# A decayed running sum over a matrix product: five of eight column slots solved pairwise with help from ScalarE and GpSimd

## The chip, the cores and the metric

The kernel runs on one core of one Trainium2 chip. The metric is device time of one execution in microseconds (us); lower is better. Engines in the profile's names: PE is TensorE (PEld its weight loads), DVE is VectorE, ACT is ScalarE, POOL is GpSimd, SP is SyncE, which only issues transfers here.

## The reference

x has 16 sequences of 2048 rows of 1024 numbers, w is 1024 x 1024, decay has one factor per column, all in fp32.

```python
def reference(x, w, decay):
    B, S, D = x.shape                 # 16, 2048, 1024
    xw = x @ w
    out = np.zeros_like(xw)
    out[:, 0, :] = xw[:, 0, :].copy()
    for t in range(1, S):
        out[:, t, :] = decay[None, :] * out[:, t - 1, :] + xw[:, t, :]
    return out.astype(np.float32)
```

Each output column is a recurrence over the 2048 rows of a sequence: the new value is the decay times the last one plus an element of the matrix product.

## The kernel before

A *chunk* is 512 rows of one sequence (64 chunks in all). The columns are handled with a row index t along the free dimension and columns along the 128 partitions, four blocks of 32 columns (one of each quarter of the 1024, index q) making up a *slot* n; there are 8 slots (K = 8), and also 8 blocks of the contraction, index k.

- `load` (L103) brings a chunk of x from memory on GpSimd's queue, cast to bf16 on the way, in four pieces of 256 KB, one per quarter q, into one of four xb buffers.
- `turn` (L112) transposes the chunk on VectorE in 32 x 32 blocks, as fp32 words that hold two bf16, into xt (four buffers), so that the contraction lies on the partitions.
- `load_w` (L77 to L90) loads w in fp32 on SP's and ScalarE's queues, and the decay behind it on the same two queues (L82); VectorE casts the even k into wsb, ScalarE the odd ones.
- `matmul` (L129): for each slot and chunk, 8 matmuls of 128 x 128 weights by 512 columns accumulate into a PSUM tile ps. PSUM has four tiles of 1024 fp32 per partition.
- `scan` (L141): VectorE runs the recurrence over the whole tile with one scan instruction, from PSUM into so. Its initial value is the last element of the tile before, which ScalarE copies to `keep` (L151).
- `back` (L156): VectorE transposes so in 32 x 32 blocks into the output tile ot (two buffers), so that rows lie on the partitions again. The back of a slot is put off until after the next slot's scan (`pending`, `flush`).
- `store` (L166): when all 8 slots of a group are in ot, SP issues four transfers, one per quarter, of 1024 KB each.

The work is done in *groups*: two groups of a single chunk, 30 groups of two chunks, two groups of a single chunk. In a two-chunk group a tile is 1024 rows long, and each slot has 16 matmuls. The next group's two chunks are turned after the scans of slots 1 and 5, and behind each turn one more chunk is loaded. In group 0 the loop over k is outside of the one over slots, so that matmuls can start when the first block of w is there. The order on each engine is the program's, except where the language's scheduler moves an instruction; nothing is pinned.

Of the kernel before, what the change touches and what calls it, by code (L numbers as in the profile page):

```python
# [9 lines left out]
FP32 = mybir.dt.float32  # L10
BF16 = mybir.dt.bfloat16
ALU = mybir.AluOpType


def _ap(ap_obj: bass.AP, new_ap, extra_offset=0):
    return dataclasses.replace(
        ap_obj,
        ap=[list(p) for p in new_ap],
        offset=ap_obj.offset + extra_offset,
    )  # L20
# [4 lines left out]
@with_exitstack  # L25
def kernel(
    ctx: ExitStack,
    tc: tile.TileContext,
    x: bass.AP,
    w: bass.AP,  # L30
    decay: bass.AP,
    out: bass.AP,
):

    nc = tc.nc
    B, S, D = x.shape
    assert w.shape == (D, D)

    NQ = 4
    P = 32
    CQ = D // NQ  # L50
    K = CQ // P
    M = K // 2
    TL = 512
    NJ = TL // P
    NC = S // TL

    const = ctx.enter_context(tc.tile_pool(name="const", bufs=1))
    xbp = ctx.enter_context(tc.tile_pool(name="xbp", bufs=4))
    xtp = ctx.enter_context(tc.tile_pool(name="xtp", bufs=4))
    sop = ctx.enter_context(tc.tile_pool(name="sop", bufs=3))  # L60
    otp = ctx.enter_context(tc.tile_pool(name="otp", bufs=2))
    psp = ctx.enter_context(tc.tile_pool(name="psp", bufs=4, space=bass.MemoryType.PSUM))

    def quad(q):
        return slice(q * P, (q + 1) * P)

    def queue(q):
        return nc.sync if q < 2 else nc.scalar

    dec = const.tile([128, K], FP32, name="dec")  # L70
    wsb = const.tile([128, K, K, NQ, P], BF16, name="wsb")

    def load_w():
        wf = otp.tile([128, M, 2 * D], FP32, name="ot")
        for m in range(M):
            for q in (0, 2, 1, 3):
                queue(q).dma_start(  # L77
                    out=wf[quad(q), m],
                    in_=_ap(w, [[2 * D, P], [1, 2 * D]], (q * CQ + m * 2 * P) * D))
        with nc.allow_non_contiguous_dma(reason="a vector of 1024"):  # L80
            for q in range(NQ):
                queue(q).dma_start(  # L82
                    out=dec[quad(q), :], in_=_ap(decay, [[1, P], [P, K]], q * CQ))
        for k in range(K):
            dst = wsb[:, k].rearrange("p n q i -> p q n i")
            src = wf.rearrange("p m (e q n i) -> p (m e) q n i", e=2, q=NQ, n=K)[:, k]
            if k % 2:
                nc.scalar.copy(out=dst, in_=src)  # L88
            else:
                nc.vector.tensor_copy(out=dst, in_=src)  # L90

    chunks = [(b, c * TL) for b in range(B) for c in range(NC)]
    nch = len(chunks)
    xt_of = {}
    xb_of = {}

    def load(c):
        if c >= nch:
            return
        b, t0 = chunks[c]  # L100
        xb = xbp.tile([128, NJ, CQ], BF16, name="xb")
        for q in range(NQ):
            nc.gpsimd.dma_start(  # L103
                out=xb[quad(q)],
                in_=_ap(x, [[D, P], [P * D, NJ], [1, CQ]], (b * S + t0) * D + q * CQ))
        xb_of[c] = xb

    def turn(c):
        xt = xtp.tile([128, M, TL, 2], BF16, name="xt")
        src = xb_of.pop(c).rearrange("p j c -> p (j c)").bitcast(FP32)  # L110
        dst = xt.rearrange("p m t e -> p (m t e)").bitcast(FP32)
        nc.vector.transpose(  # L112
            out=dst.rearrange("p (m j i) -> p j m i", m=M, i=P),
            in_=src.rearrange("p (j m c) -> p j m c", m=M, c=P))
        xt_of[c] = xt

    groups = [[0], [1]] + [[c, c + 1] for c in range(2, nch - 2, 2)] + [[nch - 2], [nch - 1]]
    for g in groups:
        assert chunks[g[0]][0] == chunks[g[-1]][0]

    last = {}
    pending = []

    def flush():
        while pending:
            pending.pop(0)()

    def matmul(ps, n, k, xt):
        nc.tensor.matmul(  # L129
            out=ps,  # L130
            lhsT=wsb[:, k, n].rearrange("p q i -> p (q i)"),
            rhs=xt[:, k // 2, :, k % 2],
            start=(k == 0),
            stop=(k == K - 1),
        )

    def scan(g, n, ps, ot):
        b, t0 = chunks[g[0]]
        T = TL * len(g)
        so = sop.tile([128, T], FP32, name="so")  # L140
        nc.vector.tensor_tensor_scan(  # L141
            out=so,
            data0=dec[:, n:n + 1].to_broadcast([128, T]),
            data1=ps,
            initial=0.0 if t0 == 0 else last[n],
            op0=ALU.mult,
            op1=ALU.add,
        )
        if t0 + T < S:
            keep = const.tile([128, 1], FP32, name=f"keep{n}", bufs=2)  # L150
            nc.scalar.copy(out=keep, in_=so[:, T - 1:T])  # L151
            last[n] = keep
        flush()

        def back():
            nc.vector.transpose(  # L156
                out=ot[:, :, n * P:(n + 1) * P],
                in_=so.rearrange("p (i t) -> p i t", t=P))

        pending.append(back)  # L160

    def store(g, ot, n0, n1, queues):
        b, t0 = chunks[g[0]]
        T = TL * len(g)
        for q in (0, 2, 1, 3):
            queues(q).dma_start(  # L166
                out=_ap(out, [[D, P], [P * D, T // P], [1, (n1 - n0) * P]],
                        (b * S + t0) * D + q * CQ + n0 * P),
                in_=ot[quad(q), :, n0 * P:n1 * P])

    load(0)
    load_w()
    load(1)
    load(2)
    load(3)
    turn(0)
    next_load = 4
    for gi, g in enumerate(groups):
        T = TL * len(g)
        ot = otp.tile([128, T // P, CQ], FP32, name="ot")  # L180
        xts = [xt_of.pop(c) for c in g]
        after = groups[gi + 1] if gi + 1 < len(groups) else []
        at = {1: after[:1], 5: after[1:]}
        final = gi + 1 == len(groups)
        if len(g) == 1:
            pss = [psp.tile([128, 2, TL], FP32, name="ps") for _ in range(K // 2)]
            if gi == 0:
                order = [(n, k) for k in range(K) for n in range(K)]
            else:
                order = [(n, k) for n in range(K) for k in range(K)]  # L190
            for n, k in order:
                matmul(pss[n // 2][:, n % 2], n, k, xts[0])
        for n in range(K):
            if len(g) == 1:
                ps = pss[n // 2][:, n % 2]
            else:
                ps = psp.tile([128, T], FP32, name="ps")
                for k in range(K):
                    for l in range(2):
                        matmul(ps[:, l * TL:(l + 1) * TL], n, k, xts[l])  # L200
            scan(g, n, ps, ot)
            for c in at.get(n, []):
                turn(c)
                load(next_load)
                next_load += 1
            if final and n == K // 2:
                pending.append(lambda: store(g, ot, 0, K // 2, queue))
        if final:
            flush()
            store(g, ot, K // 2, K, queue)  # L210
        else:
            pending.append(lambda g=g, ot=ot: store(g, ot, 0, K, lambda q: nc.sync))


# [28 lines left out]
```

## Time and profile before

| | us |
|---|---|
| time, median of 3 runs (lowest to highest) | 1050.16 (1049.74 to 1050.61) |
| the profiled execution | 1049.7 |
| its span, first to last instruction | 1047.9 |
| busy: PE, DVE | 934.0, 1000.2 |
| busy: ACT, POOL | 32.7, 163.4 |
| mean granted TensorE clock (share of full) | 0.987 |
| bytes moved by DMA, mean rate | 206.19 MB, 197 GB/s |

Busy time is the time in which an engine executed something; matmuls overlap one another, so a busy PE is not a PE at its peak, and the distance between the starts of two neighbours says more than the duration of one. Lines of the profile name the source line, the engine, the operation and the tiles (output <- inputs), and for a group of instructions the count, the busy time, the mean duration, and the idle time in front of them with what ended it.

### The profile page before, as it was taken

Reading aid. Unit: us, or ns where it says so; the run is one execution under the profiler, and the core shown is the slowest. Engines: PE = TensorE matmul, PEld = TensorE weight load, DVE = VectorE, ACT = ScalarE, POOL = GpSimd, SP = SyncE. Lnnn points to the kernel's source line nnn. Section 1 sums busy time; section 2 is a strip of 40 time slices with the busy share of each in tenths; the row PEclk is TensorE's granted clock in tenths of the full one; section 3 lists DMA queues with packets and bytes.
Section 4 is the critical chain, followed back from the end, with each engine's and each line's share of the span. In section 5 each row is a group of like instructions: output and inputs, shape, how many; then the busy total and the mean of one; then the engine's idle time right before and its main releaser. Section 6 shows DMA issues by size and latency. Waiting matters only on the chain.

```text
span 1047.9 us, 9953 instructions
## 1 busy us (share of the span) xinstructions
PE 934.0 (89%) x4015; PEld 391.9 (37%) x4096; DVE 1000.2 (95%) x612; ACT 32.7 (3%) x149; POOL 163.4 (16%) x260
## 2 busy tenths in 40 slices
PE   0869999999999999999999999999999999999990
PEld 0324444433333443333443333344333344333340
DVE  0699999999999999999999999999999999999995
ACT  1000000000000000000000000000000000000000
POOL 2401111101111100111101111110111110010000
PEclk9989999999999999999999999999999999999996
DMA  9998997999999999999999999999999999998558
GB/s 212 185 167 158 186 223 159 207 204 222 207 190 196 200 204 211 215 201 190 197 203 207 223 199 195 190 206 204 220 210 192 195 198 204 206 220 182 132 128 221
DMA packets 272430, 206.19 MB, mean 197 GB/s; under 512 B 7680, under 2 KB 271872, under 8 KB 271872
## 3 DMA queue, kind: packets, MB, share of 16 engines
q1 hardware_dynamic: 134176, 135.28, 54.9%
q0 software_dynamic: 135168, 67.13, 48.4%
q10 hardware_dynamic: 3040, 3.15, 1.3%
q8 instruction: 32, 0.52, 0.2%
q14 instruction: 14, 0.11, 0.0%
HBM read 138.42 MB, written 134.22 MB: 260 GB/s over the span
## 4 chain that ended last, share of the span: by engine, by line
DMA 51%; DVE 22%; issue 17%; POOL 6%; PE 3%; DVEq 0%; SPq 0%; POOLq 0%
DMA xb<-in_x_dram 50%; DVE ot L156 9%; DVE xt L112 7%; POOL xb L103 6%; DVE so L141 5%; PE ps L129 3%; DMA out_dram<-ot 2%; SPq L166 0%; DVEq L156 0%; DVEq L112 0%; POOLq L238 0%; DVEq L238 0%; DVEq L141 0%; POOLq L227 0%
## 5 line engine op out<-in xcount | busy, mean ns | idle before, releaser
L129 PE MATMUL ps<-xt,wsb 128*128 128x512 bf16 x4015 | 934.0, 388 | 90.2 <-DVE so L141 54.2
L129 PEld LDWEIGHTS <-wsb 128*128 128x128 bf16 x4096 | 391.9, 96 | 631.8 <-issue 100.9
L156 DVE STREAM_TRANSPOSE ot<-so 128x1024 f32<-128x1024 f32 (+1 forms) x272 | 316.0, 1175 | 6.0 <-DMA out_dram<-ot 5.9
L141 DVE TENSOR_TENSOR_SCAN so<-dec,keep,ps 128x1024 f32<-128x1024 f32 (+1 forms) x144 | 309.9, 2155 | 1.1 <-PE ps L129 1.1
L141 DVE TENSOR_TENSOR_SCAN so<-dec,ps 128x1024 f32<-128x1024 f32 (+1 forms) x128 | 282.5, 2209 | 3.5 <-PE ps L129 3.5
L103 POOL DMA_DIRECT2D xb<-in_x_dram x256 | 163.2, 645 | 762.3 <-DVE xt L112 731.9
L112 DVE STREAM_TRANSPOSE xt<-xb 128x2048 f32<-128x2048 f32 x64 | 145.8, 2301 | 18.5 <-DMA xb<-in_x_dram 18.5
L151 ACT COPY keep<-so 128x1 f32<-128x1 f32 x144 | 27.6, 191 | 969.8 <-DVE so L141 969.8
L90 DVE CAST wsb<-ot 128x1024 bf16<-128x1024 f32 x4 | 2.6, 680 | 12.0 <-DMA ot<-in_w_dram 12.0
L88 ACT CAST wsb<-ot 128x1024 bf16<-128x1024 f32 x4 | 3.9, 1041 | 0.0
L88 ACT ACT_TABLE_LOAD x1 | 1.3, 1283 | 17.5 <-DMA ot<-in_w_dram 17.5
L227 POOL MEMSET const-float32-0.0<- 128x1 f32 x1 | 0.1, 98 | 0.2 <-issue 0.2
L227 POOL MEMSET const-bfloat16-1.0<- 128x1 bf16 x1 | 0.1, 101 | 0.0
L227 POOL MEMSET const-float32-1.0<- 128x1 f32 x1 | 0.1, 98 | 0.0
L227 POOL MEMSET const-uint8-127<- 128x1 uint8 x1 | 0.1, 98 | 0.0
## 6 DMA issues: line engine op xcount, KB each, us to landing
out_dram<-ot SPq DMA_DIRECT2D x120, 1024.0 KB, 15.2
xb<-in_x_dram POOLq DMA_DIRECT2D x256, 256.0 KB, 18.8
out_dram<-ot SPq DMA_DIRECT2D x12, 512.0 KB, 8.1
ot<-in_w_dram ACTq DMA_DIRECT2D x8, 256.0 KB, 8.9
ot<-in_w_dram SPq DMA_DIRECT2D x8, 256.0 KB, 8.7
out_dram<-ot SPq DMA_DIRECT2D x4, 256.0 KB, 3.3
out_dram<-ot ACTq DMA_DIRECT2D x4, 256.0 KB, 4.0
dec<-in_decay_dram SPq DMA_DIRECT2D x2, 1.0 KB, 7.6
```

Source lines behind the costliest of these rows:

```text
L88: nc.scalar.copy(out=dst, in_=src)
L90: nc.vector.tensor_copy(out=dst, in_=src)
L103: nc.gpsimd.dma_start(out=xb[quad(q)], in_=_ap(x, [[D, P], [P * D, NJ], [1, CQ]], (b * S + t0) * D + q * CQ))
L112: nc.vector.transpose(out=dst.rearrange("p (m j i) -> p j m i", m=M, i=P), in_=src.rearrange("p (j m c) -> p j m c", m=M, c=P))
L129: nc.tensor.matmul(out=ps, lhsT=wsb[:, k, n].rearrange("p q i -> p (q i)"), rhs=xt[:, k // 2, :, k % 2], start=(k == 0), stop=(k == K - 1),)
L141: nc.vector.tensor_tensor_scan(out=so, data0=dec[:, n:n + 1].to_broadcast([128, T]), data1=ps, initial=0.0 if t0 == 0 else last[n], op0=AL ...
L151: nc.scalar.copy(out=keep, in_=so[:, T - 1:T])
L156: nc.vector.transpose(out=ot[:, :, n * P:(n + 1) * P], in_=so.rearrange("p (i t) -> p i t", t=P))
L227: nc = _bacc.Bacc("TRN2", target_bir_lowering=False, num_devices=1)
```

## The change

The recurrence is y[t] = d y[t-1] + v[t]. For five of the eight slots (n = 0, 1, 3, 4, 6; not in the last group) it is solved in pairs: with z = d v[even] + v[odd], the odd elements follow y[odd] = d^2 y[odd before] + z, a scan of half the length, and the even ones follow from them, y[even] = d y[odd before] + v[even].

- ScalarE copies the PSUM tile to xs in SBUF and writes its even elements times d to h; GpSimd adds h to the odd elements of xs; VectorE scans these 512 with d^2, which lies in PSUM (`dec2`), into every second element of so.
- Then ScalarE multiplies the scanned elements by d, and GpSimd adds the even elements of xs into the gaps of so.
- The paired slot's scan is issued one slot later, its back two slots later. The other three slots scan from PSUM as before.
- so has four buffers instead of three and two elements more in front; PSUM has three tiles of 1024 instead of four, and one tile for d^2. In group 0 only the slots 0 to 5 run with k outside; 6 and 7 follow.
- w is loaded on GpSimd's queue, behind chunk 0, and cast to bf16 by the transfer; the casts on VectorE and ScalarE become bf16 copies that reorder it. decay is loaded on ScalarE's queue, in the program behind its casts; its square is computed on VectorE in front of turn(0).
- Pieces of x are issued one or, while more than four wait, two per slot, from a list (`loads`); the turns come after slots 1 and 4.
- Every instruction but the stores' transfers is pinned: each engine's order is that of the program.

```diff
+    pin = tc.keep_in_program_order
+    PAIRED = (0, 1, 3, 4, 6)
+    TURNS = (1, 4)
-    psp = ctx.enter_context(tc.tile_pool(name="psp", bufs=4, space=bass.MemoryType.PSUM))
+    psp = ctx.enter_context(tc.tile_pool(name="psp", bufs=3, space=bass.MemoryType.PSUM))
+    pdp = ctx.enter_context(tc.tile_pool(name="pdp", bufs=1, space=bass.MemoryType.PSUM))
...
+    dec2 = pdp.tile([128, 512], FP32, name="dec2")
...
+    def load_dec():
...
+            for q in range(NQ):
+                pin(nc.scalar.dma_start(
+                    out=dec[quad(q), :], in_=_ap(decay, [[1, P], [P, K]], q * CQ)))
+        pin(nc.vector.tensor_tensor(out=dec2[:, 0:K], in0=dec, in1=dec, op=ALU.mult))
...
     def load_w():
-        wf = otp.tile([128, M, 2 * D], FP32, name="ot")
+        wb = otp.tile([128, M, 2 * D], BF16, name="ot")
         for m in range(M):
-            for q in (0, 2, 1, 3):
-                queue(q).dma_start(
-                    out=wf[quad(q), m],
+            for q in range(NQ):
+                pin(nc.gpsimd.dma_start(
+                    out=wb[quad(q), m],
...
+        def decayed(self, src):
+            h = tmp.tile([128, self.T // 2], FP32, name="h", bufs=4)
+            pin(nc.scalar.activation(
+                out=h, in_=src, func=mybir.ActivationFunctionType.Copy,
+                scale=dec[:, self.n:self.n + 1]))
+            return h
+
+        def pair(self):
+            if not self.paired:
+                return
+            T = self.T
+            self.xs = tmp.tile([128, T], FP32, name="xs", bufs=3)
+            pin(nc.scalar.copy(out=self.xs, in_=self.ps))
+            g = self.decayed(self.ps[:, 0:T:2])
+            if self.prev is None:
+                pin(nc.gpsimd.memset(self.so[:, 1:2], 0.0))
+            else:
+                pin(nc.scalar.copy(out=self.so[:, 1:2], in_=self.prev))
+            pin(nc.gpsimd.tensor_tensor(
+                out=self.xs[:, 1:T:2], in0=g, in1=self.xs[:, 1:T:2], op=ALU.add))
+
+        def scan(self):
+            T, n, so = self.T, self.n, self.so
+            if self.paired:
+                pin(nc.vector.tensor_tensor_scan(
+                    out=so[:, 3:T + 2:2],
+                    data0=dec2[:, n:n + 1].to_broadcast([128, T // 2]),
+                    data1=self.xs[:, 1:T:2],
+                    initial=0.0 if self.prev is None else self.prev,
...
+            else:
+                pin(nc.vector.tensor_tensor_scan(
+                    out=so[:, 2:T + 2],
...
+                    data1=self.ps,
...
+
+        def complete(self):
+            T, so = self.T, self.so
+            if self.paired:
+                h = self.decayed(so[:, 1:T + 1:2])
+                pin(nc.gpsimd.tensor_tensor(
+                    out=so[:, 2:T + 2:2], in0=h, in1=self.xs[:, 0:T:2], op=ALU.add))
+            if self.keep is not None:
+                pin(nc.scalar.copy(out=self.keep, in_=so[:, T + 1:T + 2]))
...
+    for q in range(NQ):
+        load(0, q)
     load_w()
+    load_dec()
+    for c in range(1, 4):
+        for q in range(NQ):
+            load(c, q)
     turn(0)
...
+    def feed(step, after):
+        for at, c in zip(TURNS, after):
+            if step == at:
+                turn(c)
+                loads.extend((next_load, q) for q in range(NQ))
+                next_load += 1
+        for _ in range(2 if len(loads) > NQ else 1):
+            if loads:
+                load(*loads.pop(0))
+
+    def behind(new):
+        if new is not None:
+            new.pair()
+        before = waiting[-1] if waiting else None
+        if before is not None and before.paired:
+            before.scan()
+        if new is not None and not new.paired:
+            new.scan()
+        if before is not None:
+            before.complete()
+        waiting.append(new)
+        if len(waiting) == 4:
+            waiting.pop(0)
+        for tl, lag in ((waiting[0] if len(waiting) == 3 else None, True),
+                        (before, False)):
+            if tl is not None and tl.paired == lag:
+                tl.back()
...
+        if gi == 0:
+            heads = [psp.tile([128, 2, TL], FP32, name="ps") for _ in range(3)]
+            for k in range(K):
+                for n in range(6):
+                    matmul(heads[n // 2][:, n % 2], n, k, xts[0])
         for n in range(K):
...
+            behind(Tile(gi, n, ps, ot))
+            feed(n, after)
+    behind(None)
+    behind(None)
```

More of the change, by code (lines that the diff above doesn't have):

```diff
@@ L59 @@
     xtp = ctx.enter_context(tc.tile_pool(name="xtp", bufs=4))
-    sop = ctx.enter_context(tc.tile_pool(name="sop", bufs=3))
+    sop = ctx.enter_context(tc.tile_pool(name="sop", bufs=4))
+    tmp = ctx.enter_context(tc.tile_pool(name="tmp", bufs=2))
     otp = ctx.enter_context(tc.tile_pool(name="otp", bufs=2))
-    psp = ctx.enter_context(tc.tile_pool(name="psp", bufs=4, space=bass.MemoryType.PSUM))
+    psp = ctx.enter_context(tc.tile_pool(name="psp", bufs=3, space=bass.MemoryType.PSUM))
+    pdp = ctx.enter_context(tc.tile_pool(name="pdp", bufs=1, space=bass.MemoryType.PSUM))
@@ L64, in quad @@
     def quad(q):
         return slice(q * P, (q + 1) * P)
-    def queue(q):
-        return nc.sync if q < 2 else nc.scalar
     dec = const.tile([128, K], FP32, name="dec")
+    dec2 = pdp.tile([128, 512], FP32, name="dec2")
     wsb = const.tile([128, K, K, NQ, P], BF16, name="wsb")
-    def load_w():
-        wf = otp.tile([128, M, 2 * D], FP32, name="ot")
-        for m in range(M):
-            for q in (0, 2, 1, 3):
-                queue(q).dma_start(
-                    out=wf[quad(q), m],
-                    in_=_ap(w, [[2 * D, P], [1, 2 * D]], (q * CQ + m * 2 * P) * D))
+    def load_dec():
@@ L80, in load_w @@
         with nc.allow_non_contiguous_dma(reason="a vector of 1024"):
             for q in range(NQ):
-                queue(q).dma_start(
-                    out=dec[quad(q), :], in_=_ap(decay, [[1, P], [P, K]], q * CQ))
+                pin(nc.scalar.dma_start(
+                    out=dec[quad(q), :], in_=_ap(decay, [[1, P], [P, K]], q * CQ)))
+        pin(nc.vector.tensor_tensor(out=dec2[:, 0:K], in0=dec, in1=dec, op=ALU.mult))
+    def load_w():
+        wb = otp.tile([128, M, 2 * D], BF16, name="ot")
+        for m in range(M):
+            for q in range(NQ):
+                pin(nc.gpsimd.dma_start(
+                    out=wb[quad(q), m],
+                    in_=_ap(w, [[2 * D, P], [1, 2 * D]], (q * CQ + m * 2 * P) * D)))
@@ L84, in load_w @@
         for k in range(K):
             dst = wsb[:, k].rearrange("p n q i -> p q n i")
-            src = wf.rearrange("p m (e q n i) -> p (m e) q n i", e=2, q=NQ, n=K)[:, k]
+            src = wb.rearrange("p m (e q n i) -> p (m e) q n i", e=2, q=NQ, n=K)[:, k]
             if k % 2:
-                nc.scalar.copy(out=dst, in_=src)
+                pin(nc.scalar.copy(out=dst, in_=src))
             else:
-                nc.vector.tensor_copy(out=dst, in_=src)
+                pin(nc.vector.tensor_copy(out=dst, in_=src))
@@ L95, with load @@
     xb_of = {}
-    def load(c):
+    def load(c, q):
         if c >= nch:
@@ L100, in load @@
         b, t0 = chunks[c]
[L101 to L106, printed above, removed]
+        if q == 0:
+            xb_of[c] = xbp.tile([128, NJ, CQ], BF16, name="xb")
+        pin(nc.gpsimd.dma_start(
+            out=xb_of[c][quad(q)],
+            in_=_ap(x, [[D, P], [P * D, NJ], [1, CQ]], (b * S + t0) * D + q * CQ)))
     def turn(c):
@@ L111, in turn @@
         dst = xt.rearrange("p m t e -> p (m t e)").bitcast(FP32)
-        nc.vector.transpose(
+        pin(nc.vector.transpose(
             out=dst.rearrange("p (m j i) -> p j m i", m=M, i=P),
-            in_=src.rearrange("p (j m c) -> p j m c", m=M, c=P))
+            in_=src.rearrange("p (j m c) -> p j m c", m=M, c=P)))
         xt_of[c] = xt
@@ L121 @@
     last = {}
[L122 to L126, printed above, removed]
     def matmul(ps, n, k, xt):
-        nc.tensor.matmul(
+        pin(nc.tensor.matmul(
             out=ps,
@@ L134, in matmul @@
             stop=(k == K - 1),
[L135 to L160, printed above, removed]
@@ L172 @@
+    for q in range(NQ):
+        load(0, q)
     load_w()
-    load(1)
-    load(2)
-    load(3)
+    load_dec()
+    for c in range(1, 4):
+        for q in range(NQ):
+            load(c, q)
     turn(0)
-    next_load = 4
+    loads = [(4, q) for q in range(NQ)]
+    next_load = 5
+    def feed(step, after):
+        nonlocal next_load
+        for at, c in zip(TURNS, after):
[6 more added lines that the diff above has]
+                load(*loads.pop(0))
@@ new lines @@
+    waiting = []
+    def behind(new):
[15 more added lines that the diff above has]
+                tl.back()
@@ L182 @@
         after = groups[gi + 1] if gi + 1 < len(groups) else []
[L183 to L192, printed above, removed]
+        if gi == 0:
[3 more added lines that the diff above has]
+                    matmul(heads[n // 2][:, n % 2], n, k, xts[0])
         for n in range(K):
-            if len(g) == 1:
-                ps = pss[n // 2][:, n % 2]
+            if gi == 0 and n < 6:
+                ps = heads[n // 2][:, n % 2]
             else:
@@ L198 @@
                 for k in range(K):
-                    for l in range(2):
+                    for l in range(len(g)):
                         matmul(ps[:, l * TL:(l + 1) * TL], n, k, xts[l])
[L201 to L212, printed above, removed]
+            behind(Tile(gi, n, ps, ot))
+            feed(n, after)
+    behind(None)
+    behind(None)
 _INS = ['x', 'w', 'decay']
```

52 lines of the change are left out of this document (43 added, 9 removed).

## The prediction

> **What bounds the kernel now.** I read the page's totals first, then a window table of the steady stretch, then the waits and the order in time there. The first fence is the page; the columns of its second line are busy time, share of the span, instructions.
>
> ```profile
> span 1047.9 us, 9953 instructions
> PE 934.0 (89%) x4015; PEld 391.9 (37%) x4096; DVE 1000.2 (95%) x612; ACT 32.7 (3%) x149; POOL 163.4 (16%) x260
> ```
>
> Next, 200 to 900 us in one window (busy us and counts of each engine, then granted clock, DMA share, GB/s), and what TensorE waited for in it (us, times, longest).
>
> ```profile
> 200.00:900.00 700.00, 655.53 (x2824) 275.08 (x2881) 700.00 (x407) 16.85 (x88) 117.04 (x184) 1.00 1.07 203
> PE ps L129 <- DVE so L141: 40.9, 58, 1.4
> ```
>
> VectorE has no idle time in 700 us: it is the bound. Weight loads, one per matmul, are recorded completely (4096), so 700/2881 = 0.2430 us per matmul, and a two-chunk group of 8 slots x 16 matmuls takes 31.10 us. TensorE's only wait is for VectorE's scans to free PSUM. From the order in time (start, duration, ...):
>
> ```profile
> 463.48 25.16 PEld L129 LDWEIGHTS <-wsb 128*128 128x128 bf16 x112 [1.01 <-issue]
> 498.83 2.27 DVE L141 TENSOR_TENSOR_SCAN so<-dec,ps 128x1024 f32<-128x1024 f32 x1
> 501.00 1.23 DVE L156 STREAM_TRANSPOSE ot<-so 128x1024 f32<-128x1024 f32 x1
> 502.13 2.27 DVE L141 TENSOR_TENSOR_SCAN so<-dec,ps 128x1024 f32<-128x1024 f32 x1
> 512.11 2.29 DVE L112 STREAM_TRANSPOSE xt<-xb 128x2048 f32<-128x2048 f32 x1
> 514.30 2.33 DVE L141 TENSOR_TENSOR_SCAN so<-dec,keep,ps 128x1024 f32<-128x1024 f32 x1
> 526.58 2.33 DVE L141 TENSOR_TENSOR_SCAN so<-dec,keep,ps 128x1024 f32<-128x1024 f32 x1
> 529.95 2.33 DVE L141 TENSOR_TENSOR_SCAN so<-dec,keep,ps 128x1024 f32<-128x1024 f32 x1
> ```
>
> Starts, not durations, give VectorE's price, because instructions overlap by about 0.1 us: a scan 2.17 (501.00-498.83), 2.24 with a keep operand; a transpose back 1.13; a turn 2.19; scan plus back 3.30 or 3.37. Eight pairs and two turns are 8 x 3.335 + 4.38 = 31.06, the 31.10 again. When PSUM is free TensorE runs 112 loads in 25.16 us: (25.16-0.10)/111 = 0.2258 us each, 28.90 us per group. So a VectorE made faster saves at most 2.20 us per group, 66 us over the 30 groups, unless TensorE's own pace falls.
>
> **The change, part by part.** The prices of single operations (instructions, then total us and mean ns):
>
> ```profile
> L141 DVE TENSOR_TENSOR_SCAN so<-dec,ps 128x512 f32<-128x512 f32 x8 | 9.4, 1190 | 3.5 <-PE ps L129 3.5
> L156 DVE STREAM_TRANSPOSE ot<-so 128x512 f32<-128x512 f32 x32 | 21.9, 695 | 5.9 <-DMA out_dram<-ot 5.9
> L88 ACT CAST wsb<-ot 128x1024 bf16<-128x1024 f32 x4 | 3.9, 1041 | 0.0
> L151 ACT COPY keep<-so 128x1 f32<-128x1 f32 x144 | 27.6, 191 | 969.8 <-DVE so L141 969.8
> L103 POOL DMA_DIRECT2D xb<-in_x_dram x256 | 163.2, 645 | 762.3 <-DVE xt L112 731.9 <-DMA xb<-in_x_dram 27.7 <-DVE so L141 1.1
> ```
>
> *VectorE.* In five slots of eight a scan of 1024 becomes one of 512 (from SBUF, stride 2, factor in PSUM): 1.19 less 0.06 to 0.1 overlap, 1.13. Group: 5 x 1.13 + 3 x 2.22 + 8 x 1.13 + 4.38 = 25.7 us, below TensorE's 28.9. No row shows a scan with that stride and a PSUM factor; the bounds are 0.7 (the 512-wide transpose) and 2.2 (no gain), and I take the row of the same width.
>
> *ScalarE.* A paired slot gets a copy of 1024 (1.04), two scaled copies of 512 (0.19 + half of 0.85 = 0.62 each) and two one-element copies (0.19): 2.66. Group: 5 x 2.66 + 3 x 0.19 = 13.9 of 28.9 us; with stride 2 at double price, 20. Hidden either way.
>
> *GpSimd.* Ten adds of 512 per group and eight load issues of 0.645. No compute row of that size exists on POOL. Lower end 0.7 (the transpose), upper end 2.93 (a 1024 scan, 2.28, plus one issue, 0.645); I take 1.3, nearest to the 512 scan because that too is a two-input operation that passes 512 elements. 10 x 1.3 + 5.2 = 18.2 us, hidden; the upper end gives 34.5, not hidden, and is the rival below. The Trainium skill's "GPSIMD Engine Reference" (3.1, side-by-side cycle accounting) gives a 2048-wide fp32 add as 4497 ns, and my estimate from it is a quarter, 1.12, by which the sum would be 16.4 us per group and the total the same; no row here shows it.
>
> *The pinned order.* A paired scan now waits for ScalarE's copy and scaled copy and GpSimd's add: 1.04 + 0.62 + 1.3 = 3.0 us after TensorE's last matmul of the slot, and is issued one slot (3.61 us) late, so it is ready. Behind a wait there queue an unpaired scan, a back or a turn. By slot VectorE has 2.3, 3.3, 4.5, 2.3, 3.3, 4.5, 2.3, 3.4 us; the sum 25.7 is what counts, since TensorE has two more PSUM tiles, 7.2 us, before a late scan stops it. PSUM buffers fall from four to three: paired slots are freed by ScalarE 1.7 us after their end, the three unpaired ones about 3 us after, so I cost this at nothing; the cover is that 7.2. On POOL a load piece waits for a turn at slots 1 and 4, about 3 us; the add queued behind it belongs to the next slot's completion and is not due earlier. x pieces now go out one or two per slot rather than four after a turn, almost two groups (over 45 us) ahead of their turn. ScalarE's completion of a slot waits for VectorE's scan, and the next slot's copy is queued behind it: 1.7 + 1.3 + 1.1 + 0.8 = 4.9 of the two slots, 7.2, that it has.
>
> *DMA.* Bytes per two-chunk group: 4.19 MB out, 2.10 MB in as bf16; in 28.9 us 218 GB/s. Windows: loads alone, stores alone, both, and a pause.
>
> ```profile
> 35.00:40.00 5.00, 5.00 (x24) 2.10 (x22) 2.31 (x1) 0.00 (x0) 2.39 (x4) 1.00 1.72 184
> 1012.00:1024.00 12.00, 11.94 (x54) 4.97 (x52) 12.00 (x14) 0.96 (x5) 0.00 (x0) 1.00 0.96 206
> 524.00:536.00 12.00, 11.22 (x50) 4.68 (x50) 12.00 (x8) 0.00 (x0) 0.00 (x0) 1.00 1.23 253
> 540.00:544.00 4.00, 3.94 (x18) 1.72 (x18) 4.00 (x4) 0.19 (x1) 0.00 (x0) 1.00 0.59 80
> ```
>
> Mixed traffic reaches 253, and there are pauses at 80. One after the other the transfers would need 4.19/0.206 + 2.10/0.184 = 31.8 us, fully mixed 24.9. Loads spread over the group are mixed with the store, so I take the mixed end: a store in about 23 us of 28.9, hidden. Its next user, the back of slot 0 two groups on, comes some 35 us after the issue.
>
> *The start.* w leaves SP's and ScalarE's queues and stands in POOL's behind x0, ahead of x1 to x3; decay's four loads stand on ScalarE behind its four casts, and turn(0) on VectorE behind the product of decay.
>
> ```profile
> 18.84 3.88 ACT L88 CAST wsb<-ot 128x1024 bf16<-128x1024 f32 x4
> DMA to landing us min/median/max: 6.2/7.2/8.4
> out_dram<-ot SPq DMA_DIRECT2D x4, 256.0 KB, 3.3
> 26.34 2.31 DVE L112 STREAM_TRANSPOSE xt<-xb 128x2048 f32<-128x2048 f32 x1 [12.94 <-DMA xb<-in_x_dram]
> 28.71 16.03 PE L129 MATMUL ps<-xt,wsb 128*128 128x512 bf16 x63 [28.71 <-DVE xt L112]
> 69.42 30.83 PE L129 MATMUL ps<-xt,wsb 128*128 128x512 bf16 x126 [2.21 <-DVE xt L112]
> ```
>
> (The second line is decay's landing, the third the shortest landing of all.) x0 and w are 3.15 MB written; at 184 GB/s 17.1 us, plus 3.3 to land: w is there at 20.4, the last ScalarE cast done at 23 instead of 22.7. Decay issued by 25, landed 7.2 later at 32 (bounds 3.3 and 8.4); turn 2.3: first matmul at 34.7 instead of 28.7. The 63 matmuls above took 1.8 us more than 63 x 0.2258, at the start. Group 0 without a stall is 64 x 0.2258 + 1.8 = 16.3; but slots 6 and 7 and group 1 wait for PSUM tiles of two slots each, whose consumers all start together when k ends (per paired half-length slot 1.1 on ScalarE, 0.7 an add, 0.6 a scan): going through the queues by hand I get stalls of 2, 4 and 2 us, 25 with rounding. Group 1, 14.5 without a stall, has slots of 1.8 us against a chain of about 2: 16. Two-chunk groups start at 75.7, where before they got going at 69.4: the start costs 6. Bounds: no stall and decay after 3.3 us, 8 earlier than now; stalls of twice that, and decay last, 18 later.
>
> *The end.* The last long store occupies the output buffer that the last group needs:
>
> ```profile
> 1008.16 33.90 SPq L166 DMA_DIRECT2D out_dram<-ot x12
> 1030.47 1.31 DVE L156 STREAM_TRANSPOSE ot<-so 128x512 f32<-128x512 f32 x2 [5.88 <-DMA out_dram<-ot]
> ```
>
> From that store's issue to the end of the span: 1047.9 - 1008.2 = 39.7, the 22 us landing, VectorE's backlog, the last store. The last group is unpaired, so this stays.
>
> **Sum.** 75.7 + 30 x 28.90 = 942.7; its last unpaired scan and two backs 5.3, so the last long store goes out at 948.0; + 39.7 = 987.7 span. The profiled execution took 1049.7, 1.8 over its span (the median of the runs is 1050.2): 989.5, said as 990.
>
> **Rivals.** *DMA becomes the bound.* For it: the mean is 203 GB/s at share 1.07, and the serial price, 31.8, is above 28.9. Against: 253 in a mix. At 210 GB/s a group takes 30.0, the time is 990 + 30 x 1.1 = 1023; at 203, 31.0, no change (1053).
>
> *GpSimd becomes the bound (slower).* Its ten adds and eight issues stand in one queue; from (31.10-5.2)/10 = 2.6 us per add the group is longer than now. At the upper end, 2.93: 34.5, 990 + 30 x 5.6 = 1158. For it: no row shows the add. Against: it must take over twice VectorE's scan of that width.
>
> *The half scan gains nothing* at 2.2 us: VectorE 31.1 per group again; about 1056, no gain.
>
> *TensorE is quicker than 0.2258*, then VectorE's 25.7 binds: 990 - 30 x 3.2 = 894. Against: 112 loads in a row at exactly that pace, at clock 1.00. The Trainium skill's "TensorE: Matmul & The Clock Gate" (back-to-back issue gap) gives a sustained 131 ns at N=512, by which this rival would be the case; the row above disagrees. Nearer in the same direction is the start at its lower bound: 976.
>
> **How the numbers follow.** TensorE-bound, 970 to 1010: 0.63, the prediction. DMA-bound, 1010 to 1048: 0.19, of it 0.03 above 1040; DMA-bound to no change: 0.02. GpSimd the bound, slower: 0.09; the half scan without gain, slower: 0.02. Below 970 (a quicker TensorE among it, 0.02): 0.05. Faster by over 0.2% (what a measurement here can tell from no change): 0.63 + 0.19 + 0.05 = 0.87; same 0.02; slower 0.11. The range 968 to 1040 leaves out 0.04 below and 0.16 above. Of the likeliest alone, 970 to 1010, the low end is the start's lower bound and the high end its upper.
>
> **What would show it.** Right: VectorE busy near 25.7/28.9, idle before scans; weight loads 0.226 apart through the middle; adds near 1.3 us; first matmul near 35; TensorE waits at groups 0 and 1. Wrong: TensorE waiting for ScalarE or VectorE in the middle; turns waiting for x loads or backs for stores (DMA); adds over 2 us.

## The result and the profile after

The changed kernel takes 987.62 us (median of 4 runs, 987.29 to 987.84), the kernel before 1049.95 beside it: ratio 0.9407, 95% interval 0.939 to 0.9423. The profiled execution took 987.84, its span is 986.1. The first lines of its page, with the line of the chain that ended last by source line:

```profile
span 986.1 us, 11189 instructions
PE 926.9 (94%) x4015; PEld 392.6 (40%) x4096; DVE 853.3 (87%) x613; ACT 393.3 (40%) x729; POOL 581.8 (59%) x686
PE ps L133 88%; DMA out_dram<-ot 2%; DMA xb<-in_x_dram 2%; DVE so L193 1%; POOL xb L113 1%; DVE ot L213 1%; POOL ot L91 0%; POOL xs L178 0%; SPq L227 0%; DVE so L184 0%; DVE xt L121 0%; ACT h L162 0%; ACT xs L172 0%; POOL so L206 0%; DVEq L323 0%
```

VectorE's busy time fell by 147 us, the span by 62. The chain is now TensorE's for 88% of the span. The window 200 to 900 us again (busy us and counts per engine, granted clock, DMA share, GB/s), and the longest stretch of weight loads in the order in time:

```profile
200.00:900.00 700.00, 695.98 (x3040) 295.98 (x3100) 640.66 (x437) 292.97 (x521) 434.91 (x493) 1.00 1.12 218
71.84 876.10 PEld L133 LDWEIGHTS <-wsb 128*128 128x128 bf16 x3880 [0.41 <-issue]
```

3880 loads with no gap worth a line: 876.0/3879 = 0.2258 us, the pace that TensorE had before only in the stretches where it did not wait for PSUM. In the window 3100 loads stand where 2881 stood, 28.9 us per two-chunk group where there were 31.1. VectorE has 8% idle time there, GpSimd 38%, ScalarE 58%. DMA moves 218 GB/s, as the group's bytes ask.

The prices that the change brought in, by shape (count, total us and mean ns, then idle time in front and what ended it):

```profile
L178 POOL TENSOR_TENSOR xs<-h,xs 128x512 f32<-128x512 f32 x150 | 195.1, 1301 | 272.3 <-ACT so L177 100.8 <-ACT h L162 84.8 <-ACT keep L209 49.7
L206 POOL TENSOR_TENSOR so<-h,xs 128x512 f32<-128x512 f32 x150 | 195.2, 1301 | 62.0 <-ACT h L162 32.9 <-ACT keep L209 28.8
L184 DVE TENSOR_TENSOR_SCAN so<-dec,xs 128x512 f32<-128x512 f32 x75 | 91.9, 1225 | 41.3 <-POOL xs L178 20.8 <-POOL so L175 20.5
L172 ACT COPY xs<-ps 128x1024 f32<-128x1024 f32 x150 | 151.8, 1012 | 299.5 <-PE ps L133 261.8 <-POOL so L175 27.7 <-remote 10.1
L162 ACT ACTIVATE h<-so,dec 128x512 f32<-128x512 f32 x150 | 114.2, 761 | 202.5 <-DVE so L184 202.5
```

GpSimd's add takes 1.30 us, the half-width scan 1.23 (1.29 with a keep operand), so VectorE gains 1.05 us per paired slot. ScalarE's idle time ends with TensorE's matmuls and VectorE's scans: it waits for work. GpSimd's idle time ends mostly with ScalarE's results, but this costs nothing: in the window 200 to 900 us TensorE, which sets the pace, has no wait for any engine.

### The profile page after: what moved, and what is told of

The parts are those of the page before. It is cut to its first block, busy times and chain, and to the rows that moved or that the text cites. A ratio compares the mean times of both kernels' runs of the same rounds, so it can differ in the third digit from the quotient of the medians.

```text
span 986.1 us, 11189 instructions
## 1 busy us (share of the span) xinstructions
PE 926.9 (94%) x4015; PEld 392.6 (40%) x4096; DVE 853.3 (87%) x613; ACT 393.3 (40%) x729; POOL 581.8 (59%) x686
## 3 DMA queue, kind: packets, MB, share of 16 engines
q10 hardware_dynamic: 3200, 1.05, 0.5%
## 4 chain that ended last, share of the span: by engine, by line
PE 88%; issue 4%; DMA 3%; DVE 2%; POOL 2%; SPq 0%; ACT 0%; DVEq 0%; POOLq 0%
PE ps L133 88%; DMA out_dram<-ot 2%; DMA xb<-in_x_dram 2%; DVE so L193 1%; POOL xb L113 1%; DVE ot L213 1%; POOL ot L91 0%; POOL xs L178 0%; SPq L227 0%; DVE so L184 0%; DVE xt L121 0%; ACT h L162 0%; ACT xs L172 0%; POOL so L206 0%; DVEq L323 0%
## 5 line engine op out<-in xcount | busy, mean ns | idle before, releaser
L133 PE MATMUL ps<-xt,wsb 128*128 128x512 bf16 x4015 | 926.9, 389 | 49.9 <-DVE xt L121 31.6
L178 POOL TENSOR_TENSOR xs<-h,xs 128x512 f32<-128x512 f32 (+1 forms) x165 | 206.3, 1250 | 293.4 <-ACT so L177 101.9
L172 ACT COPY xs<-ps 128x1024 f32<-128x1024 f32 (+1 forms) x165 | 160.6, 973 | 324.0 <-PE ps L133 285.7
L206 POOL TENSOR_TENSOR so<-h,xs 128x512 f32<-128x512 f32 (+1 forms) x165 | 206.2, 1250 | 71.7 <-ACT keep L209 37.5
L162 ACT ACTIVATE h<-so,dec 128x512 f32<-128x512 f32 (+1 forms) x165 | 122.0, 740 | 222.6 <-DVE so L184 222.6
L184 DVE TENSOR_TENSOR_SCAN so<-dec,xs 128x512 f32<-128x512 f32 (+1 forms) x80 | 95.3, 1191 | 56.4 <-POOL xs L178 35.8
L184 DVE TENSOR_TENSOR_SCAN so<-dec,keep,xs 128x512 f32<-128x512 f32 (+1 forms) x85 | 103.5, 1218 | 34.1 <-POOL xs L178 32.3
L193 DVE TENSOR_TENSOR_SCAN so<-dec,keep,ps 128x1024 f32<-128x1024 f32 (+1 forms) x59 | 122.0, 2069 | 0.5 <-PE ps L133 0.5
L162 ACT ACTIVATE h<-ps,dec 128x512 f32<-128x512 f32 (+1 forms) x165 | 111.2, 674 | 0.0
L193 DVE TENSOR_TENSOR_SCAN so<-dec,ps 128x1024 f32<-128x1024 f32 (+1 forms) x48 | 105.3, 2194 | 0.0
L177 ACT COPY so<-keep 128x1 f32<-128x1 f32 x85 | 16.3, 192 | 0.0
```

Of the source, the lines that this page charges most:

```text
L133: pin(nc.tensor.matmul(out=ps, lhsT=wsb[:, k, n].rearrange("p q i -> p (q i)"), rhs=xt[:, k // 2, :, k % 2], start=(k == 0), stop=(k == K ...
L162: pin(nc.scalar.activation(out=h, in_=src, func=mybir.ActivationFunctionType.Copy, scale=dec[:, self.n:self.n + 1]))
L172: pin(nc.scalar.copy(out=self.xs, in_=self.ps))
L177: pin(nc.scalar.copy(out=self.so[:, 1:2], in_=self.prev))
L178: pin(nc.gpsimd.tensor_tensor(out=self.xs[:, 1:T:2], in0=g, in1=self.xs[:, 1:T:2], op=ALU.add))
L184: pin(nc.vector.tensor_tensor_scan(out=so[:, 3:T + 2:2], data0=dec2[:, n:n + 1].to_broadcast([128, T // 2]), data1=self.xs[:, 1:T:2], init ...
```

## The experiments

**How many pairs it takes.** Three kernels change the line `PAIRED = (0, 1, 3, 4, 6)` and nothing else.

```diff
-    PAIRED = (0, 1, 3, 4, 6)
+    PAIRED = ()                          # e1; (1, 4) in e2; (0, 1, 2, 3, 4, 5, 6, 7) in e3
```

> All eight slots scan whole from PSUM; everything else of the change stays (pinned order, w by the casting transfer, spread loads, three PSUM tiles). Theory A, the gain is VectorE's relief alone: VectorE needs 8 x 3.35 + 4.4 = 31.2 us per two-chunk group again, 30 x 2.3 = 69 over the changed kernel, so 1050 to 1058, no faster than the kernel before. Theory B, the order and the spread loads (which mix with the stores) bring a good part: 990 to 1030.

> Slots 1 and 4 paired instead of five. Theory A: VectorE 25.7 + 3 x 1.09 = 29.0 us per group, just TensorE's 28.9: 988 to 995, so that two pairs are worth as much as five. Theory C, the pinned queues need VectorE's slack to absorb their waits: each wait shows, 1000 to 1025.

> All slots paired (the last group still is not). Theory A: VectorE 22.4, ScalarE 21, GpSimd 16 x 1.30 + 8 x 0.66 = 26.1 us per group, all below TensorE's 28.9: 985 to 992. Theory C, the chain ScalarE-GpSimd-VectorE-ScalarE-GpSimd of paired slots in a row does not fit the slot's 3.6 us: TensorE waits for ScalarE to free PSUM, above 1000.

Measured, as ratios to the kernel before: no pairs 1054.1 us (1.0036, 1.0021 to 1.0051, a little slower), two 988.7 (0.9415, 0.94 to 0.9429), five 0.9407, eight 990.65 (0.9432, 0.9416 to 0.9447). The middle window, first without pairs:

```profile
200.00:900.00 700.00, 654.95 (x2830) 275.62 (x2887) 700.00 (x407) 17.14 (x89) 114.81 (x180) 1.00 1.04 202
```

With two pairs:

```profile
200.00:900.00 700.00, 695.98 (x3039) 295.97 (x3100) 700.00 (x437) 129.34 (x266) 249.00 (x312) 1.00 1.13 218
```

With eight:

```profile
200.00:900.00 700.00, 695.98 (x3039) 296.02 (x3100) 577.14 (x437) 458.72 (x776) 622.89 (x676) 1.00 1.12 218
```

Without pairs VectorE is full (third figure with a count) and TensorE back at 2887 loads: order, spread loads and the way of w bring nothing in the middle by themselves. With two pairs VectorE is still full, and TensorE already at its 3100: both engines are saturated at once, about where 8 x 3.35 + 4.4 less 2 x 1.05, 29.1 us, meets 28.9. The last three of the five pairs only make slack. With eight the middle is again 3100 loads, though GpSimd is busy for 89% of it; what it loses against five, 3 us, lies outside the window. Theory A held in all three; theory B (e1) and theory C (e2, e3) fell here.

**What the pinning is worth.** Two kernels drop it.

```diff
-    pin = tc.keep_in_program_order
+    def pin(i):                          # e4: no instruction pinned
+        return i
...
-        pin(nc.vector.transpose(
+        tc.keep_in_program_order(nc.vector.transpose(     # e9 only: the turns alone
```

> The changed kernel without the pinning; the program's text is the same. Theory A: the order does not matter as long as VectorE has 3 us of slack per group: 985 to 995. Theory C, the written order is what keeps the chain off TensorE's path: a scheduler that moves scans, backs or adds makes it slower, above 1000.

> As the run without pinning, but the turns alone are pinned behind what stands before them on VectorE. Theory G, that run lost its time to turns that the scheduler put a whole group too early, where each waits for TensorE to finish reading the xt buffer while the scans that TensorE needs queue behind it: without that, 988 to 1010. Theory H, the scrambled order of copies, adds and scans on ScalarE and GpSimd costs as much: above 1100.

Not pinned: 1345.42 us (1.2807, 1.2788 to 1.2826). Only the turns pinned: 1021.28 (0.9723, 0.9709 to 0.9738). The order in time of the unpinned run, around one stall; the first line is TensorE's matmuls from 594.69 on:

```profile
594.69 28.69 PE L134 MATMUL ps<-xt,wsb 128*128 128x512 bf16 x121
623.19 4.51 DVE L122 STREAM_TRANSPOSE xt<-xb 128x2048 f32<-128x2048 f32 x2 [9.99 <-PE ps L134]
627.62 3.46 DVE L214 STREAM_TRANSPOSE ot<-so 128x1024 f32<-128x1024 f32 x3
631.00 1.19 DVE L185 TENSOR_TENSOR_SCAN so<-dec,xs 128x512 f32<-128x512 f32 x1
632.11 2.26 DVE L194 TENSOR_TENSOR_SCAN so<-dec,ps 128x1024 f32<-128x1024 f32 x1
634.42 6.02 PE L134 MATMUL ps<-xt,wsb 128*128 128x512 bf16 x14 [11.04 <-DVE so L194]
```

Two turns stand one behind the other, early: VectorE idles 9.99 us until TensorE's matmuls have ended (594.69 + 28.69 = 623.4) and the xt buffer they read is free. Behind the turns queue the scans that would free PSUM; the first that does so starts at 632.11, and TensorE, out of tiles, idles 11.04 us. In the window 200 to 900, 16.4 groups long (2105 loads), there are 17 such waits:

```profile
PE ps L134 <- DVE so L194: 188.6, 17, 11.2
DVE xt L122 <- PE ps L134: 168.5, 17, 10.0
```

Pinning the turns alone takes 324 of the 358 us away; the rest, 34 us, goes with the order of the other instructions, gains and losses together. TensorE's waits in the same window of that run:

```profile
PE ps L134 <- DVE so L194: 30.4, 23, 2.1
```

In e4 theory C held: the written order is what keeps these waits off TensorE's path. In e9 theory G holds for most of the loss, not all: 1021 lies above its 1010.

**GpSimd's share.** Extra adds into a scratch tile that nothing reads.

```diff
+            idle = tmp.tile([128, T // 2], FP32, name="idle", bufs=2)
+            pin(nc.gpsimd.tensor_tensor(                     # e5 and e10: ahead of the pair's add
+                out=idle, in0=g, in1=self.xs[:, 1:T:2], op=ALU.add))
...
+                pin(nc.gpsimd.tensor_tensor(                 # e5 only: ahead of the completing add
+                    out=idle, in0=h, in1=self.xs[:, 0:T:2], op=ALU.add))
```

> Each of GpSimd's ten adds per two-chunk group is preceded by one more of the same inputs into a scratch tile that nothing reads: GpSimd needs 20 x 1.30 + 8 x 0.66 = 31.3 us per group, 2.4 above TensorE's pace. The prediction's rival, GpSimd as the bound, priced: 988 + 30 x 2.4 = 1060 (1050 to 1072). If the chain matters and not the sum (each paired slot's result comes 2.6 us later): above 1075. If GpSimd's work is hidden whatever its length: 986 to 992.

> One extra add of 1.30 us per paired slot, ahead of the one that the scan waits for (the doubled adds had one there and one before the second add, and cost 117 us where the sum of GpSimd's work gave 72). GpSimd's sum is 15 x 1.30 + 8 x 0.66 = 24.8 us per group, below 28.9. If the sum decides: 986 to 992. If the longer chain counts by itself, each scan coming 1.3 us later: TensorE waits, 995 to 1030.

Doubled: 1104.75 us (1.0526, 1.0509 to 1.0544). One more per slot: 993.47 (0.9458, 0.9444 to 0.9473). The middle window of the doubled one, and what GpSimd still waits for in it:

```profile
200.00:900.00 700.00, 639.44 (x2687) 266.02 (x2740) 567.42 (x386) 253.56 (x461) 655.67 (x652) 0.97 1.01 194
```

```profile
POOL idle L210 <- ACT h L162: 18.3, 11, 1.9
POOL idle L210 <- ACT keep L215: 16.7, 11, 1.5
```

What ScalarE and VectorE wait for there:

```profile
ACT h L162 <- DVE so L187: 438.6, 108, 7.5
DVE so L187 <- POOL xs L181: 50.9, 54, 1.0
```

With one more add:

```profile
200.00:900.00 700.00, 700.00 (x3102) 295.98 (x3100) 640.08 (x436) 298.73 (x521) 592.62 (x616) 1.00 1.12 218
```

With one more add the middle is untouched (3100 loads at 85% of GpSimd): the 1.3 us longer chain is covered there. Of the 6 us that the run loses 5 are at the start, where the long stretch of loads begins at 76.82 instead of 71.84; so 993.47 falls between the two ranges that were expected.

With all adds doubled the time lies 33 us above the range that GpSimd's sum gave, and in the range of the chain. A group takes 128 x 700/2740 = 32.7 us, not the 31.3 of the sum. GpSimd is busy 655.67 of 700 us (94%), and its gaps end when ScalarE's h and keep arrive, which in turn wait for the scans of a VectorE that waits for GpSimd. Read so, GpSimd is the bound and its sum only a lower bound, because its queue feeds itself over two other engines. That the full queue does this, and not the longer chain by itself, is argued and not shown: no run lengthens the chain by 2.6 us with GpSimd half idle.

**The square's place.** `dec2` in SBUF instead of PSUM.

```diff
-    dec2 = pdp.tile([128, 512], FP32, name="dec2")
+    dec2 = const.tile([128, 512], FP32, name="dec2")
```

> The squared decay lies in SBUF instead of PSUM, so that a paired scan reads two SBUF operands; nothing else changes. Theory A: a scan's price does not depend on where that operand lies, 986 to 990. Theory D: the Trainium skill (SBUF - State Buffer, the section on ports) says that a VectorE instruction with two SBUF inputs and a GpSimd instruction that reads SBUF shut each other out for their whole length. Worked from this case's durations: five scans of 1.2 us and ten adds of 1.3 us per group in each other's way, VectorE 25.7 + up to 5 x 1.3 = 32 us: 995 to 1080, with longer scans or adds in the profile.

988.27 us (0.9412, 0.9398 to 0.9426): no difference in time. But the scans are longer:

```profile
L184 DVE TENSOR_TENSOR_SCAN so<-dec,keep,xs 128x512 f32<-128x512 f32 x75 | 120.5, 1607 | 15.9 <-POOL xs L178 14.1
L184 DVE TENSOR_TENSOR_SCAN so<-dec,xs 128x512 f32<-128x512 f32 x75 | 119.2, 1589 | 14.4 <-POOL so L175 9.7 <-POOL xs L178 4.7
```

1.59 against 1.23 us, 1.61 against 1.29. The middle window:

```profile
200.00:900.00 700.00, 695.98 (x3040) 296.02 (x3100) 676.85 (x437) 292.83 (x520) 435.69 (x495) 1.00 1.12 218
```

VectorE is busy 676.85 of 700 us in the middle instead of 640.66, and the adds keep their 1.3 us. The means hide two kinds of scan. From the order in time, one with no add running as it begins, then an add and a scan that begins during it:

```profile
304.65 1.18 DVE L184 TENSOR_TENSOR_SCAN so<-dec,xs 128x512 f32<-128x512 f32 x1
314.83 1.30 POOL L206 TENSOR_TENSOR so<-h,xs 128x512 f32<-128x512 f32 x1
314.91 2.30 DVE L184 TENSOR_TENSOR_SCAN so<-dec,keep,xs 128x512 f32<-128x512 f32 x1
```

The second scan ends at 317.21, 1.08 us after the add's end at 316.13. Of the 120 half scans that begin in the window, 72 begin with no add running and take 1.18 to 1.29 us; 48 begin during an add and take 1.97 to 2.30, always 1.07 to 1.09 more than what is left of the add. With the factor in PSUM 48 scans also begin during an add, and they take 1.22 to 1.29. So the scan waits for the running add to end, as the Trainium skill's "SBUF - State Buffer" (Who interferes with whom) lets expect for two SBUF inputs beside a GpSimd instruction that reads SBUF. Whether an add would wait for a running scan no run shows, because no add begins during one. Theory D is right on the mechanism and wrong on its price: only two scans in five meet an add, VectorE's group grows by 1.5 us to 28.0, and that costs nothing as long as it stays below TensorE's 28.9. Theory A is right on the time alone.

**The loads' spacing.**

```diff
-        for _ in range(2 if len(loads) > NQ else 1):
+        for _ in range(len(loads) if step in TURNS else 0):
```

> The four pieces of a chunk are issued together right behind its predecessor's turn, as in the kernel before, instead of one or two per slot. If the transfers have room (prediction, 24.9 us fully mixed against 28.9): 986 to 992. If spreading them over the store is what makes them fit: backs wait for stores or turns for x, 995 to 1020.

990.39 us (0.9429, 0.9413 to 0.9444), with 3100 loads in the middle: the transfers have room either way. The 2.8 us that it loses are at the start, where the long stretch of loads begins at 75.26 instead of 71.84. Spreading the loads is not where the gain came from.

**The start and the end.** e7 moves decay to SP's queue and its square and turn(0) ahead of w's copies; e8 gives the last group an output tile of its own; e12 is e7 with the last pair of chunks split in two groups.

```diff
-                pin(nc.scalar.dma_start(                   # in load_dec; e7 and e12
+                pin(nc.sync.dma_start(
...
+    load_dec()                                             # e7 and e12
+    turn(0)
     load_w()
-    load_dec()
     for c in range(1, 4):
         for q in range(NQ):
             load(c, q)
-    turn(0)
...
-        ot = otp.tile([128, T // P, CQ], FP32, name="ot")  # e8; fin is a pool of one buffer
+        pool = fin if gi + 1 == len(groups) else otp
+        ot = pool.tile([128, T // P, CQ], FP32, name="fin" if pool is fin else "ot")
...
-    groups = [[0], [1]] + [[c, c + 1] for c in range(2, nch - 2, 2)] + [[nch - 2], [nch - 1]]
+    groups = [[0], [1]] + [[c, c + 1] for c in range(2, nch - 4, 2)] + [[c] for c in range(nch - 4, nch)]   # e12
```

> Decay is loaded on SP's queue at the very start, and its square and turn(0) stand in VectorE's program ahead of w's copies. Theory A, TensorE-bound throughout, so that a start earlier by so much ends earlier by so much: matmuls follow w's blocks as they come, the first 48 end near 24 us instead of 44.4; GpSimd's twelve x issues, which end at 27.4, hold the first add back by 2: 18 us saved, 967 to 973. Rival: the start is hidden by something else (transfers that are needed anyway, the last stores): 982 to 988.

> The last group's output gets a buffer of its own, so that its first transpose back need not wait for the last long store. Theory E, the tail is that wait: VectorE's 6.2 us and TensorE's 4.9 us of idle time there go, 978 to 982. Theory F, the tail is the stores themselves: after the last long store is issued 8.4 MB are still to be written, at 206 GB/s 41 us, as long as the tail is now (41.6): 985 to 989.

> The early start of before, and the last pair of chunks worked as two single-chunk groups, so that the last four groups store 2.1 MB each. If the tail is the stores that are still to be written when the last long group ends: about 30 us after that group's 4.2 MB shrink to the last 2.1 MB behind TensorE's last matmul, 8 to 10 us off the early start's 971.5: 959 to 966. If the tail is VectorE's work and waits in the last group: 969 to 973.

The early start takes 971.53 us (0.9252, 0.9238 to 0.9265). From its order in time, matmuls at the start and the long stretch:

```profile
14.09 13.54 PE L133 MATMUL ps<-xt,wsb 128*128 128x512 bf16 x48 [14.09 <-DVE wsb L100]
55.45 876.10 PEld L133 LDWEIGHTS <-wsb 128*128 128x128 bf16 x3880 [0.23 <-issue]
```

The stretch of 3880 loads has the same length to a hundredth and begins 16.4 us earlier; the time falls by 16.1. That is what a chain of TensorE from end to end means: whatever is gained ahead of it arrives at the end. The gain is 16 us and not the 18 that were expected, because the first 48 matmuls end at 27.6 instead of 24.

The own buffer takes 990.11 us (0.9428, 0.9414 to 0.9442), no gain. VectorE's wait for the store is gone, and its last transposes end at 973.3 instead of 979.3, but the stores run on. Theory E falls. Theory F fits, but is not shown: 990.11 lies a little above its range, the tail is 43.3 us long, and SP issues the last four stores only after a pause:

```profile
972.03 1.28 DVE L214 STREAM_TRANSPOSE fin<-so 128x512 f32<-128x512 f32 x2
979.66 4.88 SPq L228 DMA_DIRECT2D out_dram<-fin  x4
```

What holds SP until 979.66 was not tested; the profile names transfers out of the same tile. So it is open how much of the tail is the bytes, and how much the order in which their stores are issued.

With the end in single groups on top of the early start, 969.74 us (0.923, 0.9216 to 0.9243); the gain over e7, 1.8 us, is not the 8 to 10 that were expected and not clear of the two intervals. It fits the range of the rival, VectorE's work and waits. The profile shows a part of why the expectation failed: the second single group now needs the buffer of the last long store:

```profile
922.13 1.90 DVE L213 STREAM_TRANSPOSE ot<-so 128x512 f32<-128x512 f32 x3 [3.69 <-DMA out_dram<-ot]
926.52 30.67 PE L133 MATMUL ps<-xt,wsb 128*128 128x512 bf16 x128 [2.10 <-DVE so L193]
```

The wait moved from the last group to the second of the single ones, and it still stops TensorE. e12 has the lowest median of all, e7 is the one whose gain is explained.

## Why the prediction was right, point by point

Predicted 990, measured 987.62. The order in time gives each term of the sum (profiled execution; the start of the changed kernel):

```profile
21.14 2.18 ACTq L83 DMA_DIRECT2D dec<-in_decay_dram  x4
29.22 2.31 DVE L121 STREAM_TRANSPOSE xt<-xb 128x2048 f32<-128x2048 f32 x1
31.58 12.82 PE L133 MATMUL ps<-xt,wsb 128*128 128x512 bf16 x48 [31.58 <-DVE xt L121]
45.39 1.97 PE L133 MATMUL ps<-xt,wsb 128*128 128x512 bf16 x7 [1.00 <-ACT h L162]
50.96 1.97 PE L133 MATMUL ps<-xt,wsb 128*128 128x512 bf16 x8 [3.60 <-ACT h L162]
55.50 44.73 PE L133 MATMUL ps<-xt,wsb 128*128 128x512 bf16 x185 [2.57 <-DVE so L193]
944.51 35.67 SPq L227 DMA_DIRECT2D out_dram<-ot  x12
966.72 0.71 DVE L213 STREAM_TRANSPOSE ot<-so 128x512 f32<-128x512 f32 x1 [6.22 <-DMA out_dram<-ot]
```

| term | predicted | measured |
|---|---|---|
| first matmul | 34.7 | 31.6 |
| group 0, stalls of | 25, 2 + 4 + 2 | 23.9, 1.0 + 3.6 + 2.6 |
| group 1 | 16 | 16.3 |
| two-chunk groups start | 75.7 | 71.8 |
| from there to the issue of the last long store | 872.3 | 872.7 |
| from that to the end of the span | 39.7 | 41.6 |
| span | 987.7 | 986.1 |

The start was forecast 3.9 us too long and the tail 1.9 too short. That the sum misses by only 1.6 is in part luck, because the two errors have opposite signs.

- *The bound and its successor.* Right: VectorE left the path, TensorE's 0.2258 us took it, to the fourth digit. That the saving is the distance between the two paces and not the 147 us of VectorE's busy time is what e2 shows most plainly.
- *The engines' work.* Per two-chunk group VectorE was forecast at 25.7 us, ScalarE at 13.9 and GpSimd at 18.2. Busy time in the middle window over its 24.2 groups gives 26.5, 12.1 and 18.0: the order was right, and all three lie below 28.9.
- *GpSimd's add.* 1.3 taken from the scan of the same width; 1.30 measured. The match is in part luck, because no row showed an add on POOL, and it was not needed to the digit: with half as much again the middle is the same (e10). The rival's point of decision, 2.6 us per add, was too generous: with two adds of 1.3 for each one the kernel is 5% slower than before (e5). It took GpSimd's queue as a sum and left out that GpSimd waits for ScalarE's results, 35 us in the window shown.
- *DMA.* The transfers were forecast to need 24.9 of the 28.9 us, taken from the mixed window: the 218 GB/s that TensorE's pace asks for flow, and bursts change nothing in the middle (e11). How much room is left no run shows.
- *Two-chunk stretch and covers.* The hand-overs between engines cost nothing in the middle, as said: TensorE waits for nobody there. That they depend on the order of the instructions was not costed: "the pinned order" was priced for its waits, and what its absence would do, 358 us (e4), did not occur to the prediction. It was no part of the sum, but without it the change would have been a loss.
- *The start.* Two terms were too long: decay landed in 6.0 us instead of 7.2, and its four issues were done at 23.3 rather than 25. Why 6.0 and not 7.2 was not tested. Its row among the transfers of the changed kernel (KB each, us to landing):

```profile
dec<-in_decay_dram ACTq DMA_DIRECT2D x4, 1.0 KB, 6.0
```

  Group 1's 16 was right for a wrong reason. Not a chain of 2 us per slot made it longer than 14.5: the granted clock did, after TensorE had paused. Windows around it, clock in the third column from the end:

```profile
50.00:55.00 5.00, 1.97 (x8) 0.83 (x9) 3.75 (x6) 3.09 (x10) 4.94 (x11) 1.00 1.20 151
55.00:60.00 5.00, 4.50 (x13) 1.63 (x13) 4.70 (x8) 2.65 (x9) 3.04 (x6) 0.66 1.39 188
60.00:65.00 5.00, 5.00 (x23) 2.10 (x22) 4.96 (x5) 2.27 (x8) 2.80 (x5) 1.00 0.66 152
```

  From 55.5 to 60 us 13 weight loads pass where 20 would: 7 x 0.2258 = 1.6 us of the 1.9 by which group 1 exceeds 14.5.
- *The tail.* 39.7 was copied from before with the store's landing, VectorE's backlog and the last store as its parts. The total held (41.6), and VectorE did wait for that store, 6.22 us; but the parts are not the only cause, because with that wait removed the end is no earlier (e8). The 8.4 MB that are still to be written when the last long store is issued would explain it at 206 GB/s, 41 us; this was not shown.

What stays open: why the end's split brought 1.8 us and not the few more that its earlier stores would allow, beyond the one wait shown; a third long output buffer together with it was not tried.

## What to carry to other kernels

Relieving the busiest engine is worth the distance to the next one's own pace, read from a stretch of the trace in which that next engine does not wait; here two relieved slots of eight were as good as five or eight. When work is moved onto more engines, each queue's order becomes part of the kernel: ask of every instruction that could be placed earlier (a turn whose buffer is still being read) what stands behind it. And take the sum of a loaded helper's work as a lower bound, since its own lateness may come back to it over the others (here 32.7 us per group for a sum of 31.3).

## What the runs showed of the hardware that was not expected

- A VectorE scan with both streams in SBUF that began while a GpSimd add ran took 1.97 to 2.30 us and ended 1.07 to 1.09 us after the add; with one stream in PSUM it took 1.22 to 1.29. The adds kept 1.30 (e6).
- After pauses of 3.6 and 2.6 us with few matmuls between, TensorE's granted clock was 0.66 over the next 5 us and back at 1.00 in the next window. In the unpinned run, with a pause of about 11 us in every group (17 in 16.4 groups), it was 0.86 over the middle, and 0.52 in the 6 us behind the wait shown above:

```profile
200.00:900.00 700.00, 508.15 (x2064) 207.85 (x2105) 441.77 (x303) 205.98 (x359) 299.73 (x343) 0.86 0.81 151
634.40:640.40 6.00, 5.98 (x15) 2.11 (x16) 6.00 (x5) 1.41 (x5) 2.56 (x4) 0.52 1.01 128
```

  There 14 matmuls took 6.02 us, 0.43 us each instead of 0.2258. That wait for PSUM was so paid twice, in the wait and in the slow matmuls after it.
